# Two low parts of weight blocks in every eight: ScalarE's negative and an accumulating DMA instead of VectorE's subtraction

## The chip, the cores and the metric

The kernel runs on one core of one Trainium2 chip. The metric is the device time of one execution in microseconds (us), as the median of the runs of a kernel. The profile comes from one more execution, which has a time of its own.

## The reference

A hybrid encoder trunk of two layers on 256 frames of width 2048, with 32 heads of 128 (inner width 4096), all in float32:

```
h = rms_norm(x, a_norm);  q, k, v, g = split(h @ a_w_in, 4)        # 2048 -> 4 x 4096
o = chunked attention over 64-frame chunks (8 left chunks, relative-position bias)
x = x + (o * silu(g)) @ a_w_out                                     # 4096 -> 2048
h_kv = rms_norm(x, kv_norm);  k_sh, v_sh = split(h_kv @ kv_w, 2)
logf = log_sigmoid(h_kv @ f_w + f_b);  cum = cumsum(logf)
h = rms_norm(x, b_norm);  q, g = split(h @ b_w_in, 2)
o = causal attention of q over k_sh, v_sh with the decay cum[t] - cum[s]
x = x + (o * silu(g)) @ b_w_out
return rms_norm(x, final_norm)
```

Nearly all of the work is the five products with the weights (some 335 MB of float32).

## The kernel before, in words

**Three matmuls for one.** To keep float32 accuracy with TensorE's faster float32r format, every operand is split into a high part (the value rounded to float32r) and a low part (value minus high part). A product is then high x high + high x low + low x high: the three matmuls of `mm3` (lines 165 to 167), each 128x128 weights against 128x512 columns.

**Units and blocks.** The weights are cut into units of 512 output columns. In layer A each of the 16 groups of two heads has a unit `aqk` (its q and k columns) and a unit `avg` (v and gate); then come four units `ao` of the output projection. Layer B has, for each group, a unit `bkv` and a unit `bqg`, then four units `bo`. A unit of an input projection has 2048 rows, which are 8 blocks of 256 rows (`nk == KD`); a unit of an output projection has 16 blocks. A block is one 512 KB transfer and feeds 12 matmuls (2 row tiles, 2 halves of the frames, 3 terms). There are 64 units x 8 = 512 blocks of the input projections and 128 of the output projections.

**The feed.** `Feed` brings the blocks in, in the order of use. For each block `load` (line 179) issues one DMA from SP into a tile `raw`, of which there are RAW = 3; `prepare` lets ScalarE copy `raw` to `hi` with rounding (line 198) and VectorE subtract, `lo = raw - hi` (line 199). Of `hi` and of `lo` there are SPLIT = 4 buffers each. `get` keeps four prepared blocks (DEPTH + 1) ahead of the one that is multiplied, in program order. A raw tile is free for the next load once its subtraction has ended, and a pair `hi`, `lo` is free once TensorE has done with its block. SP issues its loads in order: one that waits for a raw tile holds the next ones back.

**What else hangs on these queues.** Between the blocks of a unit, `drive` advances the attention of a group by the steps of tables such as `QK_STEPS`. Twice per group the attention turns data by `turn` (line 252): a transpose of 32x32 blocks on VectorE (line 257) into `qkY` or `sgY`, and then 16 small DMAs that GpSimd (POOL) issues in order (line 261) into `qkZ` or `sgZ`. `sgZ` is turned in the unit behind the group's own two (in layer A, in the next `aqk`; in layer B, in the next group's `bqg`); `qkZ` in the group's second unit (`avg`) in layer A, and in the next group's `bkv` in layer B. In program order the first of the 16 stands behind block 0 of the unit. POOL's queue is served in order, too.

Of the kernel before, what the change touches and what calls it, by code (L numbers as in the profile page):

```python
# [11 lines left out]
AF = mybir.ActivationFunctionType  # L12
OP = mybir.AluOpType
# [16 lines left out]
KD = D // P  # L30
# [24 lines left out]
def r32(ap):  # L55
    return ap.bitcast(F32)
# [3 lines left out]
def trunk(ctx, tc, x, x_t, a_norm, a_w_in, a_rel, a_w_out, kv_norm, kv_w, f_w, f_b,  # L60
          b_norm, b_w_in, b_w_out, final_norm, out):
    nc = tc.nc
    pe, act, dve, pool, sp = nc.tensor, nc.scalar, nc.vector, nc.gpsimd, nc.sync
# [13 lines left out]
    def big_tile(shape, dt, name):  # L77
        return big.tile(shape, dt, name=name, tag="big")
# [90 lines left out]
    class Feed:  # L169
# [16 lines left out]
        def prepare(self, begun=None):  # L186
            begun = begun or self.begin()
            if not begun:
                return
            spec, b, raw = begun  # L190
            nm, h = spec["name"], b - (spec["nk"] // KB - spec["late"])
            if 0 <= h < spec["kept"]:
                both = big_tile([P, 2, KB, UN], F32R, f"{nm}_keep{b}")
                hi, lo = both[:, 0], both[:, 1]
            else:
                hi = stream.tile([P, KB, UN], F32R, name=f"{nm}_hi{b}", tag="hi", bufs=SPLIT)
                lo = stream.tile([P, KB, UN], F32R, name=f"{nm}_lo{b}", tag="lo", bufs=SPLIT)
            self.his.append(act.activation(hi, raw, AF.Copy))  # L198
            self.splits.append(dve.tensor_sub(lo, raw, r32(hi)))  # L199
            self.ready.append((hi, lo))  # L200

        def fill(self):
# [497 lines left out]
```

## Time and profile before

| | |
|---|---|
| median of 2 runs | 1875.99 us (1872.25 to 1879.72) |
| the profiled execution | 1871.34 us, of which the profile's span is 1869.6 us |
| busy: TensorE, VectorE, ScalarE, POOL | 1842.5, 1121.7, 1005.5, 543.4 us |
| DMA | 398.41 MB moved |

The profile's page gives for each engine its busy time and share of the span, the span in 40 slices, the DMA queues, the chain of work that ended last, and groups of instructions by line with count, total and mean duration, and the idle time of the engine ahead of them with what ended most of it. PE is TensorE, DVE VectorE, ACT ScalarE, SP the queue that issues the loads; SPq is SP's own waiting. The time given for a DMA issue is from its issue to its landing. The timeline lists instructions in order of time, with start, duration and, in brackets, the idle time ahead and what ended it. Matmuls overlap in the pipeline, so the distance between two starts (0.227 us), not the duration of one (0.39 us), is what a matmul costs.

### The profile page before, as it was taken

How to read it: one execution, taken by the hardware profiler on the slowest of the kernel's cores; microseconds unless marked ns; L12 is line 12 of the kernel's file. 1: busy time of each engine (PE TensorE's matmuls, PEld its weight loads, DVE VectorE, ACT ScalarE, POOL GpSimd, SP SyncE). 2: the span in 40 equal slices, each digit the busy share in tenths (PEclk: the TensorE clock that was granted, in tenths of full speed). 3: DMA queues.
4: the chain of work that ended last, by engine and by line, in shares of the span. 5: the costliest groups of instructions: out<-in, count | busy, mean ns of one | idle time of the engine just before them, and what ended most of it. 6: DMA issues, size and time to landing. Idle time of an engine off the chain costs nothing.

```text
span 1869.6 us, 25092 instructions
## 1 busy us (share of the span) xinstructions
PE 1842.5 (99%) x8388; PEld 1528.2 (82%) x8388; DVE 1121.7 (60%) x1448; ACT 1005.5 (54%) x1690; POOL 543.4 (29%) x1130
## 2 busy tenths in 40 slices
PE   8999999999999999999999999999999999999998
PEld 6888888888888888788888888888888887887886
DVE  7666666656665666565656566666666665665554
ACT  5555556555555555454645555555555555554443
POOL 1433333333333333112103333333333333332000
PEclk9999999999999999999999999999999999999999
DMA  8766666666766766677756666666667666676664
GB/s 300 218 213 213 218 210 211 217 204 212 224 202 211 222 214 203 212 224 231 227 177 214 208 211 211 213 213 213 217 213 215 216 215 195 205 236 199 203 200 160
DMA packets 141489, 398.41 MB, mean 213 GB/s; under 512 B 30944, under 2 KB 35120, under 8 KB 140976
## 3 DMA queue, kind: packets, MB, share of 16 engines
q1 hardware_dynamic: 107024, 357.41, 60.0%
q0 software_dynamic: 34304, 39.39, 6.8%
q8 instruction: 66, 1.08, 0.2%
q14 instruction: 63, 0.52, 0.1%
q10 hardware_dynamic: 32, 0.01, 0.0%
HBM read 353.15 MB, written 4.23 MB: 191 GB/s over the span
## 4 chain that ended last, share of the span: by engine, by line
PE 86%; DMA 5%; DVE 2%; ACT 2%; POOL 2%; issue 2%; SPq 0%; ACTq 0%; POOLq 0%; DVEq 0%
PE bkv_acc L165 6%; PE bkv_acc L166 6%; PE bkv_acc L167 6%; PE avg_acc L165 6%; PE avg_acc L167 6%; PE avg_acc L166 6%; PE aqk_acc L167 5%; PE aqk_acc L165 5%; PE aqk_acc L166 5%; PE bqg_acc L165 4%; PE bqg_acc L166 4%; PE bqg_acc L167 4%; DMA sgZ<-sgY 4%; PE bo_acc L165 3%; PE bo_acc L166 3%; PE bo_acc L167 3%
## 5 line engine op out<-in xcount | busy, mean ns | idle before, releaser
L261 POOL DMA_DIRECT2D sgZ<-sgY x512 | 250.6, 497 | 471.6 <-DVE sgY L257 427.9
L261 POOL DMA_DIRECT2D qkZ<-qkY x512 | 250.9, 498 | 379.6 <-DVE oT L337 130.3
L199 DVE TENSOR_TENSOR avg_lo<-avg_raw,avg_hi 128x1024 fp32r<-128x1024 f32 x128 | 156.5, 1223 | 127.1 <-ACT avg_hi L198 127.0
L199 DVE TENSOR_TENSOR bkv_lo<-bkv_raw,bkv_hi 128x1024 fp32r<-128x1024 f32 x128 | 156.7, 1224 | 125.7 <-ACT bkv_hi L198 125.7
L198 ACT ACTIVATE bkv_hi<-bkv_raw 128x1024 fp32r<-128x1024 f32 x128 | 135.8, 1061 | 147.9 <-PE bkv_acc L167 84.6
L199 DVE TENSOR_TENSOR bqg_lo<-bqg_raw,bqg_hi 128x1024 fp32r<-128x1024 f32 x128 | 155.6, 1220 | 97.8 <-ACT bqg_hi L198 97.6
L198 ACT ACTIVATE avg_hi<-avg_raw 128x1024 fp32r<-128x1024 f32 x128 | 135.4, 1058 | 137.9 <-PE avg_acc L167 78.8
L199 DVE TENSOR_TENSOR aqk_lo<-aqk_raw,aqk_hi 128x1024 fp32r<-128x1024 f32 x128 | 155.0, 1219 | 83.6 <-ACT aqk_hi L198 83.5
L165 PE MATMUL aqk_acc<-aqk_hi,xTh 128*128 128x512 f32 x512 | 201.7, 394 | 2.7 <-ACT aqk_hi L198 2.7
L165 PE MATMUL bkv_acc<-bkv_hi,xkvh 128*128 128x512 f32 x512 | 200.3, 395 | 3.1 <-DVE gs L364 3.0
L165 PE MATMUL bqg_acc<-bqg_hi,xbh 128*128 128x512 f32 x512 | 201.0, 393 | 0.0
L165 PE MATMUL avg_acc<-avg_hi,xTh 128*128 128x512 f32 x512 | 200.8, 392 | 0.0
L167 PE MATMUL aqk_acc<-aqk_hi,xTl 128*128 128x512 f32 x512 | 200.5, 392 | 0.0
L166 PE MATMUL aqk_acc<-aqk_lo,xTh 128*128 128x512 f32 x512 | 200.3, 391 | 0.0
L166 PE MATMUL bkv_acc<-bkv_lo,xkvh 128*128 128x512 f32 x512 | 200.1, 391 | 0.0
L167 PE MATMUL bkv_acc<-bkv_hi,xkvl 128*128 128x512 f32 x512 | 200.0, 391 | 0.0
L167 PE MATMUL bqg_acc<-bqg_hi,xbl 128*128 128x512 f32 x512 | 199.5, 390 | 0.0
L167 PE MATMUL avg_acc<-avg_hi,xTl 128*128 128x512 f32 x512 | 199.4, 390 | 0.0
L166 PE MATMUL avg_acc<-avg_lo,xTh 128*128 128x512 f32 x512 | 199.3, 389 | 0.0
L166 PE MATMUL bqg_acc<-bqg_lo,xbh 128*128 128x512 f32 x512 | 199.3, 389 | 0.0
L198 ACT ACTIVATE bqg_hi<-bqg_raw 128x1024 fp32r<-128x1024 f32 x128 | 134.5, 1055 | 88.9 <-PE bkv_acc L167 54.1
L198 ACT ACTIVATE aqk_hi<-aqk_raw 128x1024 fp32r<-128x1024 f32 x128 | 134.2, 1056 | 81.3 <-PE aqk_acc L167 46.3
(195 smaller groups left out, 3459.9 us busy)
## 6 DMA issues: line engine op xcount, KB each, us to landing
aqk_raw<-in_a_w_in SPq DMA_DIRECT2D x128, 512.0 KB, 4.0
avg_raw<-in_a_w_in SPq DMA_DIRECT2D x128, 512.0 KB, 4.2
bkv_raw<-in_kv_w SPq DMA_DIRECT2D x128, 512.0 KB, 4.2
bqg_raw<-in_b_w_in SPq DMA_DIRECT2D x128, 512.0 KB, 4.2
ao_raw<-in_a_w_out SPq DMA_DIRECT2D x64, 512.0 KB, 4.2
bo_raw<-in_b_w_out SPq DMA_DIRECT2D x64, 512.0 KB, 4.2
sgZ<-sgY POOLq DMA_DIRECT2D x512, 40.0 KB, 3.9
qkZ<-qkY POOLq DMA_DIRECT2D x512, 32.0 KB, 3.7
```

The lines of the kernel that those rows point to most:

```text
L165: pe.matmul(acc[t], lhs.h(k)[:, ts], hi, start=k == 0, stop=False)
L166: pe.matmul(acc[t], lhs.h(k)[:, ts], lo, start=False, stop=False)
L167: done.append(pe.matmul(acc[t], lhs.l(k)[:, ts], hi, start=False, stop=k == nk - 1))
L198: self.his.append(act.activation(hi, raw, AF.Copy))
L199: self.splits.append(dve.tensor_sub(lo, raw, r32(hi)))
L261: pool.dma_start(out=z[j * SQ:(j + 1) * SQ, i], in_=y[i * SQ:(i + 1) * SQ, j])
```

## The change

In the input projections (`nk == KD`), for blocks 2 and 6 of each unit's eight, `lo` is made in another way: ScalarE writes `-hi` into `lo`, and POOL then issues a DMA that adds `raw` to it in place. The other blocks and all blocks of the output projections are as before. The line numbers behind line 199 rise by 4.

```diff
             self.his.append(act.activation(hi, raw, AF.Copy))
-            self.splits.append(dve.tensor_sub(lo, raw, r32(hi)))
+            if b % 4 == 2 and spec["nk"] == KD:
+                act.activation(lo, r32(hi), AF.Copy, scale=-1.0)
+                self.splits.append(pool.dma_start(out=lo, in_=raw, accum_op=OP.add))
+            else:
+                self.splits.append(dve.tensor_sub(lo, raw, r32(hi)))
             self.ready.append((hi, lo))
```

Which raw tile a load takes is not written in the code: the pool gives each load a tile, and the order of the program with its waits shows which. The first place is **SP's queue** at the loads of group 5's two units (the number behind `raw` is the block), before the change:

```order
L179 DMA aqk5_raw4_2247<-in_a_w_in 128x1024 [waits DMAHW6_49,DVE_49]
L179 DMA aqk5_raw5_2265<-in_a_w_in 128x1024 [waits DMAHW7_49,DVE_49]
L423 DMA tb_2393<-in_a_rel_bias 64x2x192 [waits DVE_49,Pool_49]
L423 DMA tb_2393<-in_a_rel_bias 64x2x256
L179 DMA aqk5_raw6_2283<-in_a_w_in 128x1024 [waits DMAHW0_49,DVE_49]
L179 DMA aqk5_raw7_2301<-in_a_w_in 128x1024 [waits DMAHW1_49,DVE_49]
L179 DMA avg5_raw0_2319<-in_a_w_in 128x1024 [waits DMAHW2_49,DVE_49]
```

and with the change, where a wait on DMASW is one for a DMA that POOL issued:

```order
L179 DMA aqk5_raw2_2171<-in_a_w_in 128x1024 [waits DMAHW3_49,DMASW3_49]
L179 DMA aqk5_raw3_2224<-in_a_w_in 128x1024 [waits DMAHW5_49,DVE_49]
L179 DMA aqk5_raw4_2268<-in_a_w_in 128x1024 [waits DMAHW6_49,DVE_49]
L427 DMA tb_2416<-in_a_rel_bias 64x2x192 [waits DVE_49,Pool_49]
L427 DMA tb_2416<-in_a_rel_bias 64x2x256
L179 DMA aqk5_raw5_2286<-in_a_w_in 128x1024 [waits DMAHW7_49,DMASW4_49,Activation_49]
L179 DMA aqk5_raw6_2304<-in_a_w_in 128x1024 [waits DMAHW0_49,DVE_49]
...
L179 DMA avg5_raw2_2383<-in_a_w_in 128x1024 [waits DMAHW7_49,DVE_49]
L179 DMA avg5_raw3_2425<-in_a_w_in 128x1024 [waits DMAHW5_49,DMAHW2_49,DMASW5_49]
L179 DMA avg5_raw4_2462<-in_a_w_in 128x1024 [waits DMAHW3_49,DMAHW0_49,DVE_49]
L179 DMA avg5_raw5_2480<-in_a_w_in 128x1024 [waits DMAHW1_49,DMASW6_49,Activation_49]
```

Every load waited for VectorE (its raw tile's subtraction); now four loads of a group wait for an accumulating DMA instead. POOL's DMAs take eight semaphores in turn; aqk5's block 2 has number 4, its block 6 number 5, avg5's block 2 number 6, the block 6 of the avg unit ahead number 3. So the raw tile of aqk5's block 2 goes to block 5 (3 loads on), that of its block 6 to avg5's block 3 (5 on), that of avg5's block 2 to its block 5 (3 on), and that of an avg unit's block 6 to block 2 of the next aqk (4 on). From group 2 on it is so in every group of layer A; from group 1 on layer B has 3, 4, 3 and 5, with the 5 behind block 6 of bqg.

The second place is **ACT's queue** in the same unit, first before:

```order
L198 ACTIVATE aqk5_hi5_2267<-aqk5_raw5_2265 128x1024
L198 ACTIVATE aqk5_hi6_2285<-aqk5_raw6_2283 128x1024
L198 ACTIVATE aqk5_hi7_2303<-aqk5_raw7_2301 128x1024
L198 ACTIVATE avg5_hi0_2321<-avg5_raw0_2319 128x1024
L198 ACTIVATE avg5_hi1_2339<-avg5_raw1_2337 128x1024
```

and now:

```order
L198 ACTIVATE aqk5_hi5_2288<-aqk5_raw5_2286 128x1024
L198 ACTIVATE aqk5_hi6_2306<-aqk5_raw6_2304 128x1024
L200 ACTIVATE aqk5_lo6_2307<-aqk5_hi6_2306 128x1024
L198 ACTIVATE aqk5_hi7_2325<-aqk5_raw7_2323 128x1024
L198 ACTIVATE avg5_hi0_2343<-avg5_raw0_2341 128x1024
```

The negative stands right behind the copy of its block; nothing else of ACT's order moves here.

The third place is **POOL's queue** over one group of layer A, with the change (before, the rows of line 201 are not there, and the turns and the memset follow each other):

```order
L201 DMA aqk10_lo2_4244<-aqk10_raw2_4241 128x1024
L430 MEMSET tb_4486 64x2x64
L265 DMA sgZ_4321<-sgY_4319 32x320 x16
L201 DMA aqk10_lo6_4377<-aqk10_raw6_4374 128x1024
L201 DMA avg10_lo2_4456<-avg10_raw2_4453 128x1024
L265 DMA qkZ_4515<-qkY_4513 32x256 x16
L201 DMA avg10_lo6_4571<-avg10_raw6_4568 128x1024
```

In each unit the accumulating DMA of block 2 stands ahead of the unit's turn, and that of block 6 behind all 16 DMAs of it.

## The prediction

> **What bounds the kernel now.** First the busy times, then the chain that ended last (page, parts 1 and 4):
>
> ```profile
> span 1869.6 us, 25092 instructions
> ...
> PE 1842.5 (99%) x8388; PEld 1528.2 (82%) x8388; DVE 1121.7 (60%) x1448; ACT 1005.5 (54%) x1690; POOL 543.4 (29%) x1130
> ...
> PE 86%; DMA 5%; DVE 2%; ACT 2%; POOL 2%; issue 2%; SPq 0%; ACTq 0%; POOLq 0%; DVEq 0%
> ```
>
> TensorE is busy for all but 27 us of the span. VectorE, which the change relieves, has 40% to spare: a gain can be at most those 27 us (1.4%), while whatever lets TensorE wait for a block costs in full. So the question is how late blocks may come. A block is 12 matmuls; one group's timeline on PE shows their pace and where its units begin:
>
> ```profile
> 609.40 0.47 PE L165 MATMUL aqk_acc<-aqk_hi,xTh 128*128 128x512 f32 x1
> ...
> 617.01 0.39 PE L165 MATMUL aqk_acc<-aqk_hi,xTh 128*128 128x512 f32 x1
> ...
> 617.69 0.39 PE L165 MATMUL aqk_acc<-aqk_hi,xTh 128*128 128x512 f32 x1
> ...
> 632.37 0.48 PE L165 MATMUL avg_acc<-avg_hi,xTh 128*128 128x512 f32 x1
> ...
> 655.34 0.47 PE L165 MATMUL aqk_acc<-aqk_hi,xTh 128*128 128x512 f32 x1
> ```
>
> Three matmuls take 0.68 us, so a block takes 2.72 and four take 10.9. The first and last row are the starts of two groups' aqk units: 45.9 us for 16 blocks with the attention's matmuls; another stretch of four groups, between the starts of their sgZ turns, gives the mean that I use:
>
> ```profile
> 432.02 4.40 POOL L261 DMA_DIRECT2D sgZ<-sgY  x9 [6.41 <-DVE sgY L257]
> 617.69 4.40 POOL L261 DMA_DIRECT2D sgZ<-sgY  x9 [6.68 <-DVE sgY L257]
> 662.99 4.40 POOL L261 DMA_DIRECT2D sgZ<-sgY  x9 [6.41 <-DVE sgY L257]
> ```
>
> (617.69 - 432.02) / 4 = 46.4; over five (to 662.99) 46.2. I take 46.3 per group, 11.6 per four blocks. Next, the feed, in the timelines of ACT and in the loads' waits:
>
> ```profile
> 617.94 1.06 ACT L198 ACTIVATE aqk_hi<-aqk_raw 128x1024 fp32r<-128x1024 f32 x1 [1.66 <-PE aqk_acc L167]
> 620.66 1.06 ACT L198 ACTIVATE aqk_hi<-aqk_raw 128x1024 fp32r<-128x1024 f32 x1 [1.66 <-PE aqk_acc L167]
> 623.33 1.06 ACT L198 ACTIVATE avg_hi<-avg_raw 128x1024 fp32r<-128x1024 f32 x1 [1.61 <-PE aqk_acc L167]
> SPq L179 <- DVE avg_lo L199: 298.9, 123, 5.5
> L199 DVE TENSOR_TENSOR avg_lo<-avg_raw,avg_hi 128x1024 fp32r<-128x1024 f32 x128 | 156.5, 1223 | 127.1 <-ACT avg_hi L198 127.0
> L198 ACT ACTIVATE avg_hi<-avg_raw 128x1024 fp32r<-128x1024 f32 x128 | 135.4, 1058 | 137.9 <-PE avg_acc L167 78.8
> avg_raw<-in_a_w_in SPq DMA_DIRECT2D x128, 512.0 KB, 4.2
> ```
>
> ACT's copy starts when TensorE lets go of the buffer four blocks back, three blocks (8.2 us) ahead of use. Then copy 1.06 and subtraction 1.22; the load three blocks on waits for that subtraction, and lands 4.2 us later: 6.5 us of the 8.2. The feed has 1.7 us of room in a loop.
>
> **The change part by part.** *Removed:* 128 subtractions, 128 x 1.22 = 156 us of VectorE. Worth nothing on TensorE. *Added on ACT:* 128 negatives, of the form of the copy beside them, 1.06 us: 136 us in an engine that is 54% busy, but 1.06 in each chain below. *Added on POOL and the DMA engines:* 128 accumulating DMAs of 512 KB. Let A be the time from the negative's end to the landing of the sum. No such DMA is in the trace; the nearest rows are POOL's small ones and the rates of the queues:
>
> ```profile
> sgZ<-sgY POOLq DMA_DIRECT2D x512, 40.0 KB, 3.9
> DMA to landing us min/median/max: 1.7/3.9/7.0
> q1 hardware_dynamic: 107024, 357.41, 60.0%
> L261 POOL DMA_DIRECT2D sgZ<-sgY x512 | 250.6, 497 | 471.6 <-DVE sgY L257 427.9
> ```
>
> (The second is the view of the tile sgZ.) The loads' queue moves 357.41 MB in 60.0% of 1869.6 us, 319 GB/s or 1.65 us for 512 KB. Bounds, all estimates: lowest, the fastest small DMA plus the other 472 KB as a plain copy, 1.7 + 1.5 = 3.2; plain copy from the median, 3.9 + 1.5 = 5.4; the add must fetch raw and lo, so a second 1.65 makes 7.0; if issuing 128 rows instead of 32 takes POOL four times 0.497, 8.5; if writing costs a third pass, 10.2. I take **A = 7.0**, since both operands surely have to be read and nothing says that issue grows with the rows.
>
> What A holds up: the negative's block cannot finish on TensorE before it lands, and raw stays taken, so that SP's queue stands at the load that wants this tile; the loads behind it wait too. Call the time between one landing and the next, four blocks on, P. By the distances in SP's order (3, 5, 3, 4 loads in layer A; 3, 4, 3, 5 in layer B):
> - Distance 3, twice a group: the next accumulated block's load stands behind the held one. Landing, issue 0.33, load 4.2, second load behind it 1.65 - 0.33 = 1.3, copy 1.06, negative 1.06, A: P = 8.0 + A = 15.0.
> - Distance 4: it is the held load itself: 4.2 + 2.1 + 0.1 + A = 6.4 + A = 13.4.
> - Distance 5: the load is free, but the buffers hi and lo are those of the block just landed, which TensorE takes 2.72 for: 2.9 + 2.1 + A, about 5.1 + A = 12.1.
>
> Each is at least the 11.6 that TensorE needs. In the unit that turns sgZ, block 6's DMA also stands behind the turn in POOL's queue:
>
> ```profile
> 625.74 0.98 POOL L261 DMA_DIRECT2D sgZ<-sgY  x2 [0.17 <-issue]
> 667.75 3.42 POOL L261 DMA_DIRECT2D sgZ<-sgY  x7 [0.37 <-DMA sgZ<-sgY]
> ```
>
> These end 17.3 and 15.8 us after their units' starts at 609.40 and 655.34, 16.6 in the mean. Block 2 lands as TensorE comes to it, 5.4 after the unit's start, and block 6's negative ends 8.0 later, at 13.4: 3.2 us wait, in one of the two long loops. The other turn does not hold it up:
>
> ```profile
> 635.35 4.40 POOL L261 DMA_DIRECT2D qkZ<-qkY  x9 [8.62 <-DVE oT L337]
> 642.15 1.47 POOL L261 DMA_DIRECT2D qkZ<-qkY  x3 [0.20 <-issue]
> ```
>
> Its unit, avg, starts at 632.37 on PE, and the turn ends at 643.6, 11.3 after that, ahead of 13.4.
>
> Sum per group: 15.0 + 18.2 + 13.4 + 12.1 = 58.7 against 46.3, 12.4 more; times 32 is 397. The profiled execution's span 1869.6 + 397, and 1.7 around it (1871.34 was its time): 2268. It stood 4.6 under the median of the runs, so **2270** for a median. The output projections, some 390 us, stay as they are. At the bounds the same sum gives 2020 (A = 4.2, a load's own time), 2103 (5.4), 2465 (8.5) and 2682 (10.2).
>
> DMA load itself is no bound: 128 x 3.3 us of 16 engines is 23% of today's span on top of the 0.69 in the last row quoted below, and of a span that is longer then.
>
> **The rivals.**
> *Short accumulate, collision only.* A of 3.2 to 5.4: 11.6 + 14.4 + 11.6 + 11.6 = 49.2 at 3.2, 2.9 x 32 = 93 more: 1970 to 2100. For it: the fastest small DMA, and that the accumulate flies when few loads do. Against: the second operand.
> *Not slower.* A up to 3.6, and VectorE, with four subtractions fewer per group (4.9 us), gives sgY 3 us earlier, so that block 6's DMA finds POOL free. Then all loops are below 11.6 and the time is 1850 to 1876, say 1870. It decides at A = 3.6 with the turn over 13.4 us after the unit's start. Against: sgY waits for ACT's steps, which get longer. The Trainium skill's page "DMA: Bandwidth & Descriptors" (Anatomy of one DMA) fits a DMA from GpSimd as 2.0 us plus its bytes at 436 GB/s, an estimate of 3.2 us here; by that alone no loop but the one with the collision would slow down, and the sum would be 1970. No row here shows an accumulate by it, and the median of 3.9 us for 40 KB is above its 2.1.
> *Long accumulate.* A of 8.5 and more, by issue or a third pass: 2465 to 2682.
> *TensorE's clock.* Waits of several us can lower the granted clock. One place shows it:
>
> ```profile
> 1716.00:1724.00 8.00, 3.93 (x15) 3.33 (x14) 3.97 (x6) 2.59 (x5) 0.51 (x2) 0.71 0.49 159
> 609.40:656.10 46.70, 46.70 (x218) 39.03 (x217) 29.18 (x38) 25.73 (x44) 15.87 (x33) 1.00 0.69 219
> ```
>
> With PE busy 3.93 of 8 us the clock is 0.71, against 1.00 in a full group (DMA share 0.69 there): 0.29 x 8 = 2.3 us lost. In my sum this falls into the waiting, as the loops don't run over TensorE's pace. If it did not, 128 x 2.3 = 297 more, 2570. The skill's page "TensorE: Matmul & The Clock Gate" (Part 1) has the clock halved after an idle window of some 3.4 us; the row agrees in kind.
>
> **How the numbers follow.** Forecast (A 5.4 to 8.5) 0.55; short accumulate 0.18; long 0.15; clock 0.07; not slower 0.05. The range runs from 2000 to 2580: it leaves out the not-slower case, the lower third of the short one and the upper half of the long one, under 0.2. About 2% is what a measurement of this kernel can tell from no change; every case but one is slower by 5% or more: slower 0.95, within 2% 0.04, faster by more 0.01.
>
> **What would show it.** Right: SP's longest waits at line 179 name the accumulating DMA instead of VectorE; PE's busy share falls to some 80%; its waits are at line 166, for a low part made by that DMA; a group takes 58 us; the landing time of the 128 DMAs is near 7 us; ACT's negatives take 1.06. Wrong: landing below 4 us, or PE still above 97%, or waits at POOL's turns instead of SP. The qkZ and sgZ turns should keep their 0.497 us per issue.

## The result and the profile after

The changed kernel takes 2255.39 us (median of 2 runs, 2247.93 to 2262.86) against 1875.99: the ratio is 1.204, with a 95% interval of 1.198 to 1.210. The forecast was 2270. The profiled execution took 2247.93 us, its span 2246.2.

The busy times and the DMA queues on its page (parts 1 and 3; q1 carries the loads, q0 what POOL issues):

```profile
span 2246.2 us, 25320 instructions
PE 1961.9 (87%) x8388; PEld 1584.2 (71%) x8388; DVE 971.3 (43%) x1320; ACT 1135.8 (51%) x1818; POOL 666.8 (30%) x1258
q1 hardware_dynamic: 107024, 357.41, 47.8%
q0 software_dynamic: 52736, 106.51, 22.7%
```

VectorE lost 150 us of work and ScalarE gained 130, as the change says. TensorE has the same 8388 matmuls, but now stands idle for 2246.2 - 1961.9 = 284 us instead of 27, and the same matmuls keep it busy for 119 us more. So the 377 us that the span grew are 257 us of waiting and 119 us of longer work. Most of the second goes with the clock: the mean granted clock fell from 0.995 to 0.938. By the trace's records of it, 47 stretches, 282 us in all, ran at half clock; before there were 3, 19 us. TensorE was busy for 202 of the 282 us, so some 100 us of work were lost in them (an estimate: half of 202).

What TensorE waits for, and then what SP waits for (us in total, times, longest):

```profile
PE op L284 <- ACT wideh L279: 90.4, 29, 6.0
PE avg_acc L166 <- DMA avg_lo<-avg_raw: 60.8, 18, 5.4
PE aqk_acc L166 <- DMA aqk_lo<-aqk_raw: 45.1, 18, 5.1
PE bqg_acc L166 <- DMA bqg_lo<-bqg_raw: 34.4, 19, 4.4
PE bkv_acc L166 <- DMA bkv_lo<-bkv_raw: 26.5, 19, 6.3
```

```profile
SPq L179 <- DMA avg_lo<-avg_raw: 230.8, 32, 12.0
SPq L179 <- DMA bkv_lo<-bkv_raw: 219.9, 32, 14.4
SPq L179 <- DMA bqg_lo<-bqg_raw: 152.8, 32, 7.7
SPq L179 <- DMA aqk_lo<-aqk_raw: 126.2, 32, 8.9
```

Both are as predicted: TensorE waits at line 166 for low parts made by the accumulating DMA (167 us), and SP's waits at line 179 name that DMA, 730 us in all. By the matmuls of each block, 153 of the 167 us are at block 6 and 14 at block 2, which lands 0.7 to 2.0 us (means of the four units) before TensorE comes to its low part. A third wait was not in the forecast: 90 us at `op`, the attention's product that needs the turned `sgZ`.

The view of line 201, the accumulating DMA (ns min/median/max of an issue, and the landing):

```profile
L201 POOL DMA_DIRECT2D avg_lo<-avg_raw x32: 856/902/961, 40.4 to 938.4; - x32
DMA to landing us min/median/max: 4.5/5.3/10.9
```

It lands in 5.3 us in the median, not in the predicted 7. That hides a difference: the means by unit are 5.0 to 5.3 for block 2, and for block 6 6.6 (aqk), 6.2 (avg), 5.6 (bkv) and 6.7 (bqg). One group in POOL's timeline shows where block 6 loses time:

```profile
717.08 0.87 POOL L201 DMA_DIRECT2D aqk_lo<-aqk_raw  x1 [11.39 <-ACT aqk_lo L200]
...
725.86 5.95 POOL L265 DMA_DIRECT2D sgZ<-sgY  x12 [6.43 <-DVE sgY L261]
732.01 1.97 POOL L265 DMA_DIRECT2D sgZ<-sgY  x4 [0.20 <-issue]
734.47 0.92 POOL L201 DMA_DIRECT2D aqk_lo<-aqk_raw  x1 [0.49 <-DMA sgZ<-sgY]
```

and ACT's row of the negative that it waits for:

```profile
727.98 1.06 ACT L200 ACTIVATE aqk_lo<-aqk_hi 128x1024 fp32r<-128x1024 f32 x1
```

The negative ends at 729.04, in the middle of the turn, and the DMA is issued at 734.47: 5.4 us behind 16 small DMAs. The same turn five groups earlier gives the pace:

```profile
432.65 5.95 POOL L265 DMA_DIRECT2D sgZ<-sgY  x12 [6.45 <-DVE sgY L261]
```

(725.86 - 432.65) / 5 = 58.6 us per group of layer A; it was 46.4, and 58.7 was predicted. In layer B the distances between the accumulating DMAs add up to 57.5. TensorE's timeline at the end of that wait:

```profile
738.51 0.40 PE L165 MATMUL avg_acc<-avg_hi,xTh 128*128 128x512 f32 x1
741.95 0.80 PE L166 MATMUL aqk_acc<-aqk_lo,xTh 128*128 128x512 f32 x1 [3.05 <-DMA aqk_lo<-aqk_raw]
742.54 0.63 PE L167 MATMUL aqk_acc<-aqk_hi,xTl 128*128 128x512 f32 x1
742.97 0.63 PE L166 MATMUL aqk_acc<-aqk_lo,xTh 128*128 128x512 f32 x1
...
747.66 0.56 PE L165 MATMUL aqk_acc<-aqk_hi,xTh 128*128 128x512 f32 x1
748.05 0.39 PE L166 MATMUL aqk_acc<-aqk_lo,xTh 128*128 128x512 f32 x1
748.28 0.39 PE L167 MATMUL aqk_acc<-aqk_hi,xTl 128*128 128x512 f32 x1
```

Three things are to be seen. After the wait the matmuls start 0.43 us apart instead of 0.23, for 6 us. The stretch by itself, in the table by windows (the clock is the third number from the end):

```profile
742.00:748.00 6.00, 6.00 (x14) 4.79 (x15) 0.00 (x0) 1.29 (x2) 0.00 (x0) 0.50 0.51 175
```

TensorE is fully busy there and half as fast. It is one of the 47 stretches named above; all but one of them last 3.4, 6.8 or 10.2 us. And the block in front of the wait is one of `avg` although block 6 of `aqk` is not done: the scheduler now lets matmuls of the next unit, and the first `op`, stand between block 6's high and low parts on TensorE, where `op` stood behind block 7 before. The ten matmuls of `op` are cut into one and nine in this way in 29 of the 32 groups, before in none. The prediction had not looked for this.

### The profile page after: what moved, and what is told of

It is laid out like the page before. It is cut to its first block, busy times and chain, and to the rows that moved or that the text cites. A ratio compares the mean times of both kernels' runs of the same rounds, so it can differ in the third digit from the quotient of the medians.

```text
span 2246.2 us, 25320 instructions
## 1 busy us (share of the span) xinstructions
PE 1961.9 (87%) x8388; PEld 1584.2 (71%) x8388; DVE 971.3 (43%) x1320; ACT 1135.8 (51%) x1818; POOL 666.8 (30%) x1258
## 5 line engine op out<-in xcount | busy, mean ns | idle before, releaser
L166 PE MATMUL avg_acc<-avg_lo,xTh 128*128 128x512 f32 x512 | 215.2, 420 | 64.0 <-DMA avg_lo<-avg_raw 60.8
L166 PE MATMUL aqk_acc<-aqk_lo,xTh 128*128 128x512 f32 x512 | 215.0, 420 | 45.1 <-DMA aqk_lo<-aqk_raw 45.1
L166 PE MATMUL bqg_acc<-bqg_lo,xbh 128*128 128x512 f32 x512 | 215.5, 421 | 34.4 <-DMA bqg_lo<-bqg_raw 34.4
L167 PE MATMUL aqk_acc<-aqk_hi,xTl 128*128 128x512 f32 x512 | 212.0, 414 | 0.0
L167 PE MATMUL bqg_acc<-bqg_hi,xbl 128*128 128x512 f32 x512 | 211.7, 414 | 0.0
L167 PE MATMUL avg_acc<-avg_hi,xTl 128*128 128x512 f32 x512 | 209.7, 410 | 0.0
L203 DVE TENSOR_TENSOR avg_lo<-avg_raw,avg_hi 128x1024 fp32r<-128x1024 f32 x96 | 116.0, 1221 | 169.7 <-ACT avg_hi L198 169.7
L203 DVE TENSOR_TENSOR bkv_lo<-bkv_raw,bkv_hi 128x1024 fp32r<-128x1024 f32 x96 | 118.0, 1230 | 161.9 <-ACT bkv_hi L198 161.8
L203 DVE TENSOR_TENSOR bqg_lo<-bqg_raw,bqg_hi 128x1024 fp32r<-128x1024 f32 x96 | 117.5, 1224 | 162.3 <-ACT bqg_hi L198 162.3
L203 DVE TENSOR_TENSOR aqk_lo<-aqk_raw,aqk_hi 128x1024 fp32r<-128x1024 f32 x96 | 117.5, 1224 | 124.8 <-ACT aqk_hi L198 124.8
```

What stands on the lines that cost most here:

```text
L166: pe.matmul(acc[t], lhs.h(k)[:, ts], lo, start=False, stop=False)
L167: done.append(pe.matmul(acc[t], lhs.l(k)[:, ts], hi, start=False, stop=k == nk - 1))
```

## The experiments

The distances below are from one accumulating DMA's issue to the next, means over 16 groups of layer A out of POOL's timelines (15 in the last column of distances); a2 is block 2 of `aqk`, v6 block 6 of `avg`. "Behind the turn" is the mean wait between the end of block 6's negative and its DMA's issue, in aqk / avg / bkv / bqg. TensorE's pace before was 11.6 us for each of the four.

| kernel | median us | a2-a6 | a6-v2 | v2-v6 | v6-a2 | behind the turn | landing | clock |
|---|---|---|---|---|---|---|---|---|
| the change | 2255 | 17.7 | 12.9 | 14.5 | 13.5 | 5.0 / 1.9 / 0.7 / 3.6 | 5.3 | 0.938 |
| raw from HBM | 2290 | 19.2 | 11.6 | 16.0 | 13.6 | 6.7 / 3.7 / 0.8 / 6.0 | 6.3 | 0.928 |
| ahead in POOL | 2146 | 13.3 | 15.1 | 13.8 | 12.9 | 0.4 / 1.2 / 0.6 / 0.3 | 5.2 | 0.962 |
| both | 2149 | 13.3 | 15.6 | 13.0 | 13.3 | 0.6 / 2.2 / 0.4 / 0.6 | 6.6 | 0.965 |
| four raw tiles | 2231 | 18.6 | 12.2 | 14.5 | 11.9 | 6.2 / 3.5 / 1.9 / 6.2 | 5.0 | 0.934 |
| four, ahead | 2123 | 12.8 | 15.5 | 13.8 | 12.5 | 0.7 / 2.8 / 0.5 / 0.7 | 5.0 | 0.951 |
| plain copy | 2110 | 17.3 | 10.5 | 14.2 | 12.1 | 5.3 / 2.4 / 0.7 / 4.4 | 3.5 | 0.960 |

**Block 2 alone, block 6 alone.** The condition `b % 4 == 2` becomes:

```diff
-            if b % 4 == 2 and spec["nk"] == KD:
+            if b == 2 and spec["nk"] == KD:      # first run
+            if b == 6 and spec["nk"] == KD:      # second run
```

> Only block 2 of each unit's eight takes the new way (64 DMAs), block 6 goes back to VectorE. Theory (a held raw tile stops SP's queue once every four blocks, and block 6's DMA stands behind POOL's turn): the DMA of block 2 is issued ahead of the turn and there are eight blocks of 2.72 us to make good one held tile (21.8 us against a loop of 8.0 + 5.6), so nearly nothing is left: 1876 to 1900 us. Rival 1 (each accumulating DMA costs TensorE the same, by its landing time or by load on the DMA engines): half of the 379 us, about 2065. Rival 2 (ScalarE's added negatives): also half, about 2065.

> Only block 6 of each unit's eight takes the new way (64 DMAs), block 2 goes back to VectorE. Theory: no loop of held tiles (eight blocks between two), but the DMA stands behind the turn: where sgZ is turned it is issued 16.6 us after the unit's start and lands 5.3 later, at 22 instead of the 16.3 at which TensorE wants it (5.6 lost), where qkZ is turned some 1 us is lost: 32 x 6.6 = 210, about 2085 us. Rival 1 (same cost for each DMA): 2065, and the same as with block 2 alone. Rival 3 (POOL's turn doesn't matter, only the held tile): 1876 to 1900.

1962.04 us (ratio 1.047, 1.043 to 1.050) and 2205.17 (1.177, 1.173 to 1.181); before was 1874.35 beside them. Block 2 costs 88 us and block 6 331, so the place decides and not the number of DMAs. Both were expected too low. With block 6 alone its DMAs stand some 28 us apart, so the loss does not need a second accumulated block close by. It still waits 5.8, 3.9, 0.9 and 5.5 us behind POOL's turns, and its median landing is 6.4 us, against 5.2 with block 2 alone. With block 6 alone TensorE's order is the changed one, with block 2 alone the old one, so that the two runs don't tell the turn in POOL's queue from TensorE's order.

**Raw read from HBM.** The DMA adds the raw block from HBM a second time, so that no raw tile is held by it:

```diff
-                self.splits.append(pool.dma_start(out=lo, in_=raw, accum_op=OP.add))
+                self.splits.append(pool.dma_start(out=lo, in_=spec["w"][b], accum_op=OP.add))
```

> As the change, but the accumulating DMA adds the block from the weights in device memory instead of from the raw tile, so that raw is free once ScalarE has copied it. Theory: all loops of the held tile are gone (what is left is 5.1 + 5.6 = 10.7, below 11.6), the two collisions with POOL's turns stay: about the time of block 6 alone, 2085 us. Rival 1 (cost of each DMA as such): no better than the change, 2255 or more, since device memory is read once more. Rival 4 (TensorE's clock makes most of it): near 2255 as long as waits stay.

2289.76 us (1.220, 1.215 to 1.224), slower than the change. SP's waits at the accumulating DMA are gone from its list, whose first rows are now

```profile
SPq L179 <- DVE avg_lo L203: 259.0, 91, 14.1
SPq L179 <- DVE bkv_lo L203: 254.5, 90, 6.8
```

and nothing is won. This spoke against the loop through the held raw tile, though not cleanly, since the DMA itself lands 1.0 us later (6.3).

**ScalarE's negative without the DMA.** VectorE adds raw to the negative; blocks 2 and 6 have one more step on ScalarE, and nothing else changes:

```diff
-                self.splits.append(pool.dma_start(out=lo, in_=raw, accum_op=OP.add))
+                self.splits.append(dve.tensor_add(lo, raw, r32(lo)))
```

> ScalarE writes the negative in blocks 2 and 6, but VectorE adds raw to it; no accumulating DMA. Theory: the negative's 1.06 us lies in the 1.7 us of room that the feed has in a loop: 1876 us within 1%. Rival 2 (ScalarE's 136 us more in its queue, ahead of the attention's work, delay the feed): slower by 2% or more.

1926.04 us (1.027, 1.025 to 1.030): 52 us for negatives that were thought to fit into ScalarE's idle time. TensorE's waits name two steps of the attention, one made by ScalarE and one by VectorE:

```profile
PE op L284 <- ACT wideh L279: 22.4, 11, 4.4
PE bkv_acc L165 <- DVE gs L368: 16.7, 13, 2.0
```

In the kernel before the same two waits were 6.8 and 3.0 us, so they are 29 of the 52 us.

**Ahead of the turn in POOL's queue.**

```diff
-                self.splits.append(pool.dma_start(out=lo, in_=raw, accum_op=OP.add))
+                with tc.high_priority():
+                    self.splits.append(pool.dma_start(out=lo, in_=raw, accum_op=OP.add))
```

Block 6's DMA then stands behind 7 or 8 of `sgZ`'s 16 and no longer behind all of them; TensorE's order is the old one again, which is a second difference.

> As the change, with one difference: the accumulating DMA has priority when the order is made, so that block 6's stands in POOL's queue behind the first 7 of sgZ's 16 DMAs, not behind all 16. Same DMAs, same held raw tiles. Theory A (both count: the wait behind the turn, 3.6 to 5 us a group in the trace of the change, and the loops of the held tile): a group falls from 58 to about 52 us, 2020 to 2080 us. Theory B (the turn in POOL's queue is all): about what the negative alone costs, 1926 to 1960. Theory C (the DMA's latency as such): 2255.

2146.16 us (1.141, 1.139 to 1.143): 109 us less than the change, yet above what the first two theories gave. POOL's timeline shows the place:

```profile
736.32 3.50 POOL L266 DMA_DIRECT2D sgZ<-sgY  x7 [6.16 <-DVE sgY L262]
740.55 0.92 POOL L202 DMA_DIRECT2D aqk_lo<-aqk_raw  x1 [0.73 <-ACT aqk_lo L200]
741.15 3.80 POOL L266 DMA_DIRECT2D sgZ<-sgY  x7
746.62 0.99 POOL L266 DMA_DIRECT2D sgZ<-sgY  x2 [1.67 <-DMA aqk_lo<-aqk_raw]
```

The long distance a2-a6 falls from 17.7 to 13.3, but a6-v2 grows from 12.9 to 15.1. The turn now stands behind the DMA: its last two DMAs wait for that DMA's landing. So `sgZ` comes late, and in 15 of 16 groups avg's block 2 finds its copy on ScalarE behind the attention's step on `sgZ`.

**Blocks 1 and 3.** The same 128 DMAs in other places:

```diff
-            if b % 4 == 2 and spec["nk"] == KD:
+            if b in (1, 3) and spec["nk"] == KD:
```

> The same number of accumulating DMAs, but for blocks 1 and 3 of each unit, whose DMAs stand ahead of the unit's turn in POOL's queue (in layer B block 3 behind the first 2 of qkZ's 16). Theory A: the six blocks behind make good the held tiles, what is left is the negatives (52 us) and layer B's two: 1950 to 1990. Theory B: 1926 to 1960. Theory C (each DMA costs by itself): about 2255.

2065.42 us (1.098, 1.095 to 1.100): 190 us less than the change, though above what was expected. The two DMAs follow each other at 4.5 to 6 us, then comes a pause of some 20; nothing waits longer than 0.9 us in the mean behind POOL's turns. TensorE's order is the old one here too.

**Ahead in POOL, and raw from HBM.** Both edits shown above together.

> Both at once: priority in POOL's queue, and the addend read from device memory, so that no raw tile is held. Theory A: nothing is left but the negatives (1926) and a landing of 6.3 us that is 0.5 us over what three blocks cover: 1930 to 2000, at least 60 us under the run with priority alone. Theory B (the held tile never mattered): the same time as with priority alone, within 2%. Theory C: 2290 as from device memory before.

2149.24 us (1.143, 1.141 to 1.146), as with the first edit alone. Theory A's 1930 to 2000 is missed: again nothing is won by the free tile, but again the landing is longer (6.6), which may hide a gain.

**A plain copy in place of the accumulation.** The addition is left out (the low part is then raw itself); order, places and bytes written are the same:

```diff
-                self.splits.append(pool.dma_start(out=lo, in_=raw, accum_op=OP.add))
+                self.splits.append(pool.dma_start(out=lo, in_=raw))
```

> As the change, but the DMA copies raw into lo without adding (the low parts of these blocks are then the raw weights: the addition is left out). If the add's second operand takes a pass of its own (1.65 us for 512 KB at the loads' rate), the landing falls from 5.3 to some 3.7 us and the time by up to 128 x 1.6 = 205 us, 2050 to 2150. If the adding is free: 5.3 us and 2255 as before.

2110.29 us (1.123, 1.117 to 1.128), as expected if the second operand is a pass of its own. TensorE's order is that of the change, so only the DMA's issue and landing differ. The view of line 201 beside that of the change:

```profile
L201 POOL DMA_DIRECT2D avg_lo<-avg_raw x32: 530/556/577, 40.9 to 868.0; - x32
DMA to landing us min/median/max: 2.9/3.5/7.0
```

The addition costs 1.8 us of landing, of which up to 0.35 may be POOL's longer issue (0.902 - 0.556), and 145 us of the kernel's time.

**Four raw tiles.** RAW = 4, with small tiles moved into buffers of others to make room; once in the kernel before as a control, once in the change, once with the DMA ahead in POOL:

```diff
-RAW = 3
+RAW = 4
...
-        grow = small.tile([2 * KD, P], F32, name=f"grow{k0}", tag="grow", bufs=1)
+        grow = att.tile([2 * KD, P], F32, name=f"grow{k0}", tag="oT")
...
-    fb = const.tile([P, H], F32, name="fb")
+    fb = att.tile([P, H], F32, name="fb", tag="q1l")
```

> The kernel before with four raw tiles instead of three; to make room for the fourth, five small tiles of the attention and the forget gates share buffers of others. It is the control of the next two: 1876 us within 1%, since loads were not waited for.

> The change with four raw tiles (and the shared small buffers of the control). By the order of SP's loads the held tile now goes to the load 4, 6, 4 and 5 blocks on, in the place of 3, 5, 3 and 4: the two loops of 8.0 + A become 6.4 + A. If the held tile counts: 1.6 us less in two loops of a group, 32 x 3.2 = 102 less than the change, 2120 to 2190 us. If the wait in POOL's queue and the landing alone count: 2255 within 2%.

> Priority in POOL's queue and four raw tiles. If the held tile counts where POOL's turn no longer hides it: some 100 us less than with priority alone (2146), 2030 to 2090 us, as the landing of 5.2 us from a raw tile is shorter than the 6.6 from device memory that hid this before. If it doesn't: 2146 within 2%.

Before: 1878.78 us (1.000, 0.998 to 1.002), so the moved tiles cost nothing. The change: 2230.92 (1.187, 1.183 to 1.191), 24 us less. Ahead: 2122.51 (1.131, 1.128 to 1.134), 24 less than with three tiles. A fourth tile gives each load four blocks' time instead of three, and the landing is not longer here than in the change (5.0). So the fourth tile is worth about 1%, not the several loops of 12 to 15 us that the prediction built on the held tile. SP's waits for the accumulating DMA are as long with four tiles as with three (752 us against 730).

Yet in the change it is the load that ends most of the copies' waiting. The copies of `bqg` on ScalarE, first in the change, then with four tiles (busy, mean ns, idle time ahead and what ended most of it):

```profile
L198 ACT ACTIVATE bqg_hi<-bqg_raw 128x1024 fp32r<-128x1024 f32 x128 | 134.7, 1053 | 118.9 <-DMA bqg_raw<-in_b_w_in 100.0
L198 ACT ACTIVATE bqg_hi<-bqg_raw 128x1024 fp32r<-128x1024 f32 x128 | 134.0, 1055 | 116.6 <-PE bkv_acc L167 81.7
```

With four tiles the load no longer comes last, and the negative of block 6 in `bqg` ends 11.1 us after the unit's start instead of 13.9 (means). But the turn in POOL's queue ends at 17.2, as in the change (17.5), and the DMA stands behind it. In all four units the wait behind the turn grew by 1.2 to 2.6 us, about what the copies had won. With the DMA ahead in POOL the fourth tile again wins time for the copies, but TensorE's waits at `op` grow from 27 to 56 us.

What the copies of accumulated blocks wait for in the last of these kernels (four tiles, ahead), by the ACT rows of line 198: TensorE letting go of the buffer four blocks back in 12 of 16 (aqk6), 14 (bkv6), 16 (bqg2) and 15 (bqg6); the attention's step on `sgZ` in 15 and 14 of 16 (avg2, bkv2). Only avg6 still waits mostly for its load (11).

**The negative on VectorE.**

```diff
-                act.activation(lo, r32(hi), AF.Copy, scale=-1.0)
+                dve.tensor_scalar(lo, r32(hi), -1.0, None, op0=OP.mult)
```

> The change with one edit: the negative of blocks 2 and 6 is made by VectorE (the high part times -1) and not by ScalarE; the accumulating DMA, its place in POOL's queue and the result stay. ScalarE is back at 1005 us of work as before, VectorE has its 128 subtractions replaced by 128 negatives of a similar length. Theory A, the 52 us that ScalarE's negatives cost by themselves (run with the negative alone) are also in the change's time, because the copies of other blocks and the attention's steps stand behind them: 2255 - 52 = 2203, between 2180 and 2220. Theory B, the accumulated blocks come so late that ScalarE's extra microsecond lies in time in which TensorE waits anyway: 2255 within 1.5%, and the mean distances between the accumulating DMAs stay at 17.7, 12.9, 14.5 and 13.5 us in layer A. Theory C, VectorE is the worse place, since the negative then stands behind the transposes and the reductions of the attention in VectorE's queue and the accumulation starts later: 2290 or more.

2255.88 us (1.202, 1.198 to 1.206): the same as the change, theory B. Its row on VectorE:

```profile
L200 DVE TENSOR_SCALAR avg_lo<-avg_hi x32: 687/694/778, 40.5 to 945.4; 128x1024 fp32r<-128x1024 f32 x32
```

ScalarE had its 127 us back and the negative was 0.37 us shorter, and neither shows in the time; the distances stay within 0.5 us (17.8, 13.2, 15.0 and 13.3). So it makes no difference which engine writes the negative. That the negative costs nothing in the change is not shown by it, as no run leaves it out.

## Why the prediction was right, and where it was not

**Direction and size: right, the size by luck.** 2270 was given, 2255 measured; 58.7 us per group, 58.6 measured in layer A. The waits at lines 166 and 179, the negatives' 1.06 us and the turns' issue (502 and 508 ns) are as forecast, and the output projections stayed (178 us from the first to the last matmul of ao, as before). PE's busy share is 87% and not some 80%, because the slow matmuls count as busy. That the sum came within 15 us is luck: errors in it offset each other.

**A, the time to the landing: too long for block 2, nearly right for block 6.** 7.0 was taken from three terms; measured are 5.3 in the median and 0.3 between the negative and the issue, 5.6. Block 6, at which TensorE waits, takes 5.9 to 7.0 in the means of the four units, its wait behind the turn left out; no run shows why it lands later. The fixed part and the plain copy were set too high: "plain copy from the median" gave 5.4, and the run with a plain copy lands in 3.5. The price of the second operand was about right: 1.65 predicted, 1.8 measured with the longer issue in it. That it is a second pass is not shown by this. That the issue does not grow with the rows was right for the copy (0.556 us for 128 rows, 0.50 for 32); the accumulating form takes 0.90. By the Trainium skill's page "DMA: Bandwidth & Descriptors" (Anatomy of one DMA) the estimate was 3.2 us; the plain copy's fastest is 2.9 and its median 3.5, so the rule holds about for the copy and not for the accumulation. With 5.6 in the prediction's own loops the sum is 13.6 + 16.8 + 12.0 + 11.6 = 54.0 us per group, some 2120 in all: 135 us too low. With the means of each place in layer A it is 18.1 + 14.5 + 12.0 + 11.6 = 56.2 and some 2190, 60 us too low. (Both are estimates.)

**The loops of the held raw tile: there, but worth little.** The step that failed is the price put on "raw stays taken, so that SP's queue stands at the load that wants this tile". SP does stand there, 730 us long, and the four distances that were predicted (18.2, 12.1, 15.0, 13.4) look like those measured (17.7, 12.9, 14.5, 13.5; between landings, as the prediction counts, 19.2, 11.3, 15.7, 12.4). Yet with a fourth raw tile, or with raw from HBM, the distances stay what they were within 1.6 us, and the time within 1.5%; the fourth tile wins 24 of 379 us. A queue that waits for a long time sets the time only if nothing else is nearly as late. Here block 6's DMA also stands behind the turn, which takes up what the tile gives, and the copy also needs the buffers `hi` and `lo` of the block four back. The prediction saw that second chain, but only for distance 5, where it gave P = 5.1 + A. With the median landing that is 10.7 us, less than TensorE's 11.6 and therefore harmless by the prediction's reasoning.

**The clock: not in the sum.** What that reasoning left out is that TensorE takes longer for a block that lands late, at half clock up to twice its 2.7 us. From its first low part to its end, block 6 took 4.0 to 4.3 us in the mean in aqk, avg and bqg and 3.0 in bkv; block 2, nearly always at full clock, took 2.7 to 2.8. That can lengthen the distances that start at a block 6 by some 1.4 us, an estimate, and not those that start at a block 2. The prediction held that the lost clock "falls into the waiting". TensorE's busy time grew by 119 us, some 100 of them at half clock in 47 stretches of 6 us in the mean; by the prediction's way of counting each lost 3.0 us, against the 2.3 of the one stretch that it had seen. Whether these 100 us would have been waited anyway is not shown, as no run holds the clock. The Trainium skill's page "TensorE: Matmul & The Clock Gate" (Part 1) has the half clock behind an idle window of some 3.4 us. The wait of 3.05 us at 741.95 and the 0.50 at 742 agree in kind; in size the trace differs, as in the 3.4 us ahead of these stretches TensorE was busy for up to half of the time.

**The collision in POOL's queue: right in kind, its size by luck.** 3.2 us per group were predicted in the sgZ unit and none in the qkZ unit, 3.2 x 32 = 102 us. Taking block 6 out of the turn gave 109. The reckoning for the sgZ unit holds: in aqk block 6's negative ends 13.1 us after the unit's start (13.4 predicted) and the turn at 17.9 (16.6 predicted). The waits themselves are longer, 5.0 and 1.9 in layer A, 3.6 and 0.7 in layer B, and taking them away makes a new one, behind the late `sgZ` on ScalarE. TensorE's changed order went back with the same edit, so that a part of the 109 may belong to that. No run here settles it: TensorE's order is the changed one in every run with block 6's DMA behind the whole turn of `sgZ`, and in the others the old one in all but one group.

**ScalarE's negatives: wrong by themselves, open in the sum.** "1.06 in each chain" and nothing beside: alone they cost 52 us; in the change it makes no difference whether ScalarE or VectorE writes them (2255.88 with VectorE), and their own price there is not shown.

**What stays open.** How the some 244 us that are left with the DMA ahead and four raw tiles split between the hi and lo buffers, the half clock and ScalarE's queue. In the profiled executions TensorE has 102 us more of work and 150 us more of waiting there than in the kernel before; the largest waits are those at the low parts of accumulated blocks (81 us) and at `op` (56 us). Fifth buffers for `hi` and `lo` would tell more; no run has them. Open too are TensorE's order by itself and the longer landing of block 6. None of the versions with the change or a part of it is faster than the kernel before; the nearest has ScalarE's negative without any DMA, 2.7% slower.

## What to carry to other kernels

Moving work off an engine that is not the bound can win no more than the bound's idle time (27 us here), and its price is the lateness of what the bound waits for: 6.7 us instead of 1.2 (negative, issue and landing against one subtraction) in a feed with 1.7 us of room. Before a queue's long wait is called the cause, ask what else is nearly as late: one more buffer shows what that wait is worth, and a sum that comes out right doesn't. If the time stays, look for the wait that has grown in its place. Where a DMA's landing is on the path, its place counts beside its length: 128 of them cost 379 us at blocks 2 and 6, and 190 less at blocks 1 and 3.

## What the runs showed of the hardware

An accumulating DMA of 512 KB within SBUF lands in 5.3 us in the median (fastest 4.5, slowest 10.9), a plain copy of the same tiles in 3.5 (2.9), and with its source in HBM the accumulation takes 6.3 to 6.6. Issuing it takes POOL 0.90 us against 0.556 for the copy of as many rows. VectorE negates 128x1024 elements in 0.694 us, where a subtraction with two operands takes 1.22 and ScalarE's negative 1.06.
